# State-space layer: the input matrices of a pair of groups by one product of 128 rows, and value weights 424 bytes behind a multiple of 512

## The chip, the core and the metric

The kernel runs on one core of a Trainium2 chip. A core has a matrix engine (TensorE, in the profile PE; its weight loads are shown as PEld), a vector engine (VectorE, DVE), a scalar engine (ScalarE, ACT), GpSimd (POOL) and a queue that issues most DMAs (SyncE, SP). The engines run side by side and wait for each other on semaphores. Two memories matter: SBUF, 128 partitions wide, where operands lie, and PSUM, to which matmuls write and from which ACT or DVE copy the results away.

The metric is the device time of one launch in microseconds. A matmul multiplies a stationary operand (loaded first by LDWEIGHTS, partitions x columns) with a moving operand that streams through the array. A plain fp32 matmul stands in the trace as two MATMUL records and two LDWEIGHTS records; an fp32r matmul (a rounded format that the kernel uses for its high and low parts) stands as one of each.

## What is computed

Two residual layers over 512 tokens of width 1024. The first layer's mixer is a grouped state-space layer, the second's is attention with a forget gate; each is followed by a gated feed-forward part. The part of the reference that the change touches first is the state-space mixer: 64 groups of 16 channels, each with a complex diagonal state of 64.

```python
def s5_mixer(h, w_in, lam_re, lam_im, log_dt, b_re, b_im, c_re, c_im, d_skip, w_glu, w_out):
    u = h @ w_in
    ug = u.reshape(Bsz, S, S5_GROUPS, S5_GROUP)
...
    bb_re = k_re[..., None] * br - k_im[..., None] * bi
    bb_im = k_re[..., None] * bi + k_im[..., None] * br
...
        bu_re = jnp.einsum('blgc,gpc->blgp', u_c, bb_re)
        bu_im = jnp.einsum('blgc,gpc->blgp', u_c, bb_im)
...
        y = jnp.einsum('blgp,gcp->blgc', hs_re, cr) - jnp.einsum('blgp,gcp->blgc', hs_im, ci)
...
    y = y + d_skip.astype(f32) * u.astype(f32)
    y = jax.nn.gelu(y)
    y = y * jax.nn.sigmoid(y @ w_glu.astype(f32))
    return (y @ w_out.astype(f32)).astype(h.dtype)
```

The second part touched is the value projection of the attention, `v = proj[..., 2 * D_MODEL:3 * D_MODEL]`, together with the 16 forget logits that stand behind it.

## The kernel before

**The state-space layer.** The kernel does not scan token by token. It takes 8 tokens as one block (L = 8, so 64 blocks). Within a block the output is a small triangular (Toeplitz) product, and between blocks a scan over 64 steps carries the state. All of it is done for 8 groups at a time (GM = 8, 128 channels), in eight rounds m = 0 to 7. A round consists of:

- `inputs(m)`, lines 1163 to 1176: the projection u of these 128 channels, an fp32 product with 8 steps of 128x512 on PE (line 1169), a copy by ACT (line 1171), and a way through DRAM that turns its layout.
- `s5_inputs(m)`, lines 947 to 998: DVE makes the tile x (two products, lines 955, and a sum, line 959). On 128 partitions it holds a pair of groups, 64 states each: partitions 0 to 63 belong to group q, partitions 64 to 127 to group q + 4. PE then multiplies x with planes of the tile `rr` (line 971): two planes with the matrix C, and four planes with an identity matrix between them, so that one product both transposes x (the 64 columns that go to `w1`) and multiplies it with C (the 16 columns that go to `kt`). The real and imaginary part r = 0, 1 are accumulated in the 16 columns where they overlap. ACT copies the result from PSUM to `w1` (line 978) and `kt` (line 982), DVE adds the skip term to `kt` (line 983), `kt` goes to DRAM and comes back as a Toeplitz tile `tw` (lines 987 and 990), and ACT masks it into `t` (line 995).
- `s5_scan(m)`, lines 1000 to 1043: PE multiplies `w1` with u (line 1010), and DVE rotates, scans and rotates back (lines 1021 to 1042); ACT makes the scan's coefficients (line 1027).
- `s5_states_out(m)`, line 943, by `s5_outer` (line 935): DVE makes the matrices `w2` that read the states out, from `rr` too.
- `s5_outputs(m)`, lines 1045 to 1067: PE adds the products with `t` (line 1052) and with `w2` (line 1060), ACT applies the gelu (line 1066).

Beside these, PE makes the conditioning columns of this and the next sub-layer from weights that are streamed in (`ada_pe`, line 205), and from round 7 on the first four column tiles of the gate product (`glu_head`, line 1198).

The matmul of line 971 uses 64 partitions, one group at a time. `tile_position=(64 * g2, 0)` places it in the upper or lower half of the array, so that a product of the upper and one of the lower half can be under way together. For each pair of q (the loop over `a`), two PSUM tiles named `aux` are filled, one for each half. There are four `aux` tiles, and the scan, the outputs and the conditioning columns use them too. The tile x has one buffer, so DVE makes the next round's x only when line 971 has read the last one.

**What sets the order.** The start of the kernel, up to line 1159, stands in a block with a schedule by hand for PE, ACT, DVE and SP: there the order in the code is the order on each queue. `s5_planes` (line 805) and `s5_signs_c` (line 800) belong to it. Behind it the framework puts the instructions of each engine in an order, when the kernel is built, from their dependencies, its own costs and a few `issue_after` hints; on the chip each engine then works its queue in that order.

**The values of the attention.** `fox_values` (line 1322) multiplies the tokens with the value weights: here the activations are stationary and the weights move (line 1361), 256 columns for each of four parts q, and 272 for q = 0, which carries the forget logits. The weights are split by `split` into a high and a low part (lines 269 to 278). `part_of` (line 67) lays each part into a tile and leaves `aside` elements free in front of it. For the value weights that is VALUES, 16 elements or 64 bytes; other products use ASIDE, 22 elements or 88 bytes, for weights that are stationary.

Of the kernel before, what the change touches and what calls it, by code (L numbers as in the profile page):

```python
# [8 lines left out]
F32 = mybir.dt.float32  # L9
F32R = mybir.dt.float32r  # L10
I32 = mybir.dt.int32
AF = mybir.ActivationFunctionType
# [5 lines left out]
P = 128  # L18
# [4 lines left out]
G = 64  # L23
CG = 16
# [3 lines left out]
GM = P // CG  # L28
# [32 lines left out]
    pool.tile([P, n // 4], F32, name="fill", bufs=1)  # L61


ROOM, ASIDE, VALUES = 9 * P, 22, 16


def part_of(pool, shape, name, tag, bufs, aside=0):
# [714 lines left out]
class S5(Trunk):  # L782
# [16 lines left out]

    def s5_signs_c(self):  # L800
        nc = self.nc
        nc.scalar.activation(self.rr[:, 0], self.rr[:, 6], AF.Copy, scale=-1.0)
        return nc.scalar.activation(self.rr[:, 6], self.rr[:, 5], AF.Copy, scale=-1.0).ins

    def s5_planes(self, pool):
        nc = self.nc

        self.rr = pool.tile([P, 7, G // 2, CG], F32, name="s5_rr")
        eye = self.first["s5_eye"].rearrange("p (k c) -> p k c", c=CG)
        nc.scalar.activation(self.rr[:, 1:5], eye[:, :, None, :].to_broadcast([P, 4, G // 2, CG]), AF.Copy)  # L810
        self.z = self.dram.tile([KT, P + L - 1, CG * GM], F32, name="s5_z")
        self.causal = self.first["s5_causal"]
        self.mask = pool.tile([P, B], F32, name="s5_mask")
        nc.gpsimd.memset(self.mask, 1.0)
        nc.gpsimd.memset(self.mask[:, 0:1], 0.0)
# [124 lines left out]

    def s5_states_out(self, m):

        t1, t2 = self.s5_outer(m, self.er, self.rr[:, 5::-5], self.ei, self.rr[:, 0::6], ("w2", "x2"))
        self.nc.vector.tensor_tensor(t1, t1, t2, ALU.add)
        return t1

    def s5_inputs(self, m):

        nc, pool = self.nc, self.s5q

        qs = slice(m * (GM // 2), (m + 1) * (GM // 2))
        sh = [P, GM // 2, 2 * CG, L]
        x, x2 = (pool.tile([P, GM // 2, 2, CG, L], F32, name=n, bufs=1 if n == "x" else 2) for n in ("x", "x2"))
        for o, l, a in ((x, self.lr, 1), (x2, self.li, 0)):
            nc.vector.tensor_tensor(
                o.rearrange("p k r c j -> p k (r c) j"), l[:, qs, None, :].to_broadcast(sh),
                self.bb[:, qs, a:a + 2, :].rearrange("p k r c -> p k (r c)")[:, :, :, None].to_broadcast(sh), ALU.mult,
            )
        self.x_made = nc.vector.tensor_tensor(x, x, x2, ALU.add).ins
        w1 = pool.tile([P, GM, P], F32, name="w1", bufs=2)  # L960
        kt = pool.tile([P, CG, GM], F32, name="kt", bufs=2)
        dd = pool.tile([P, CG * GM], F32, name="dd", bufs=1)
        nc.sync.dma_start(dd, self.io["s5_dd"][m])
        for a in range(0, GM // 2, 2):
            ps = [self.aux.tile([P, 3, 160], F32, name="aux") for _ in range(2)]
            for j in range(2):
                q = m * (GM // 2) + a + j
                for r, (cols, planes) in enumerate(((slice(0, 80), slice(1, 6)), (slice(64, 144), slice(0, 5)))):
                    for g2 in range(2):
                        rows = slice(64 * g2, 64 * g2 + 64)  # L970
                        nc.tensor.matmul(  # L971
                            ps[g2][:, j, cols], x[rows, a + j, r].rearrange("p c j -> p (c j)"),
                            self.rr[rows, planes, q, :], start=(j == 0 and r == 0), stop=True,
                            tile_position=(64 * g2, 0), skip_group_check=True,
                        )
            for g2 in range(2):
                g = g2 * (GM // 2) + a
                nc.scalar.activation(
                    w1[:, g:g + 2, :].rearrange("p g (r x) -> p g r x", r=2),
                    ps[g2][:, :2].rearrange("p g (r x) -> p g r x", r=2)[:, :, :, :64], AF.Copy,  # L980
                )
                nc.scalar.activation(kt[:, :, g:g + 2].rearrange("p c g -> p g c"), ps[g2][:, :2, 64:80], AF.Copy)
        nc.vector.tensor_tensor(
            kt.rearrange("p c g -> p (c g)"), kt.rearrange("p c g -> p (c g)"), dd, ALU.add,
        )
        z = self.z[m]
        nc.sync.dma_start(z[:P], kt.rearrange("p c g -> p (c g)"))
        R = CG * GM
        tw = pool.tile([P, L, CG, GM], F32, name="tw", bufs=1)
        nc.sync.dma_start(  # L990
            tw.rearrange("p i c g -> p i (c g)"), bass.AP(z.tensor, z.offset, [[R, P], [R, L], [1, R]])
        )
        t = pool.tile([P, GM, CG, L], F32, name="t", bufs=3)
        for i in range(L):
            nc.scalar.activation(
                t[:, :, :, i].rearrange("p g c -> p c g"), tw[:, i], AF.Copy, scale=self.causal[:, i:i + 1]
            )
        return w1, t
# [76 lines left out]
    def s5(self, i, nxt):  # L1075
        nc, tc = self.nc, self.tc
# [4 lines left out]
        with ExitStack() as stack:  # L1081
# [7 lines left out]
            with ExitStack() as start:  # L1089
# [3 lines left out]
                def load_w(m):  # L1093
                    w[m] = self.raw([P, KT, P], self.io["s5_w_in"][m], m % 3)
# [6 lines left out]
                with tc.manual_schedule(engines={ENG.PE, ENG.Activation, ENG.DVE, ENG.SP}):  # L1101
# [3 lines left out]
                    ps = self.mm.tile([P, S], F32, name="mmp")  # L1105
# [4 lines left out]
                    rows = self.tmp.tile([P, S], F32, name="nm_t")  # L1110
# [6 lines left out]
                    scale = self.ada_pe(i, (1,), late=True)  # L1117
# [5 lines left out]
                    x = self.act.tile([P, KT, S], F32, name="a_x", tag="a_hi")  # L1123
# [6 lines left out]
                    ps = self.mm.tile([P, S], F32, name="mmp")  # L1130
# [8 lines left out]
                        nc.tensor.matmul(ps, w[0][:, k, :], x[:, k], start=(k == 0), stop=(k == KT - 1))  # L1139
                    next(shift)  # L1140
                    load_w(1)
                    nc.sync.dma_start(self.rr[:, 5:7], self.io["s5_c"])
                    nc.sync.dma_start(
                        self.z[:, P:, :].rearrange("m j r -> j m r"), zero[:, None, :].to_broadcast([L - 1, KT, CG * GM])
                    )
# [14 lines left out]
            pool = self.s5r = spool("s5r", stack)  # L1160
# [41 lines left out]
            ps = self.aux.tile([KT, P], F32, name="aux")  # L1202
            nc.tensor.transpose(ps, self.sc, self.ident)
            rows = self.tmp.tile([KT, P], F32, name="nm_h", bufs=4)
# [436 lines left out]
```

## Time and profile before

| what | us |
|---|---|
| median of three runs | 1230.08 |
| lowest, highest | 1227.98, 1237.5 |
| the profiled execution, its own time | 1229.46 |
| its span from first to last instruction | 1227.7 |
| PE busy in the span | 1192.7 (97%) |
| DVE busy | 1007.7 (82%) |
| ACT busy | 606.2 (49%) |
| state-space rounds on PE, line 971 first to last start | 48.2 to 158.5 |
| value products, line 1361 first to last start | 628.3 to 675.6 |

The table is from the first block of the profile's page, the list of runs, and the answers on the two source lines. A matmul record's duration is its whole way through the array, and records overlap, so busy time says little about how densely PE works. The chain of waits is of more use: it follows the work that ended last and gives to each piece the time until the next piece could start. The sums of the prediction are made from that view.

### The profile page before, as it was taken

The numbers are of one execution on the slowest core, as the hardware profiler recorded it, in microseconds if no ns is written. First come the engines' busy times: TensorE is split into PE (matmuls) and PEld (weight loads), VectorE is DVE, ScalarE is ACT, GpSimd is POOL, SyncE is SP. The second block draws the span as 40 slices with busy tenths as digits, with TensorE's granted clock in tenths as the row PEclk, the third lists the DMA queues.
The fourth block names the chain that finished last, engine by engine and source line by source line (L and its number), as shares of the span: only waits on it lengthen the run. The fifth ranks groups of instructions, "written<-read, shape, count | busy, mean of one in ns | idle before, by whom it ended". The sixth has DMA issues, their size and how long they took to land.

```text
span 1227.7 us, 20566 instructions
## 1 busy us (share of the span) xinstructions
PE 1192.7 (97%) x7921; PEld 1022.8 (83%) x7921; DVE 1007.7 (82%) x1872; ACT 606.2 (49%) x1137; POOL 82.7 (7%) x143
## 2 busy tenths in 40 slices
PE   7999999999999999999999999999999999999997
PEld 2466678898989899789899878778889999999987
DVE  7988886679899989799678588785899887888865
ACT  3543465336444543445443565654456554555543
POOL 0000000100000000000000333331000000000000
PEclk9999999999999999999989999999999999999999
DMA  9776678531354554453425444431313332233331
GB/s 353 241 247 215 223 220 282 192 133 44 129 173 162 189 161 154 157 174 116 144 104 205 167 135 145 156 123 62 113 47 107 119 119 91 101 104 108 108 99 69
DMA packets 74385, 183.83 MB, mean 150 GB/s; under 512 B 23231, under 2 KB 25631, under 8 KB 73263
## 3 DMA queue, kind: packets, MB, share of 16 engines
q1 hardware_dynamic: 68239, 161.02, 39.7%
q0 software_dynamic: 5760, 20.97, 5.2%
q8 instruction: 62, 1.02, 0.3%
q10 hardware_dynamic: 288, 0.52, 0.1%
q14 instruction: 36, 0.29, 0.1%
HBM read 175.57 MB, written 6.92 MB: 149 GB/s over the span
## 4 chain that ended last, share of the span: by engine, by line
PE 60%; issue 26%; DVE 8%; DMA 3%; POOL 1%; ACT 1%; SPq 0%; DVEq 0%; POOLq 0%; ACTq 0%
PE mmp L294 24%; PE mmp L550 10%; PE mmp L1169 4%; PE aux L550 4%; PE mmp L1361 2%; DVE w_lo L278 2%; PE aux L971 2%; PE mmp L1198 2%; POOL ada_raw L233 1%; PE aux L1060 1%; PE aux L1500 1%; PE mmp L205 1%; PE aux L1052 1%; DMA ada_raw<-in_ada_t 1%; PE mmp L1109 1%
## 5 line engine op out<-in xcount | busy, mean ns | idle before, releaser
L278 DVE TENSOR_TENSOR w_lo<-raw,w_hi 128x1024 fp32r<-128x1024 f32 (+4 forms) x173 | 183.3, 1065 | 31.7 <-ACT w_hi L277 31.3
L277 ACT ACTIVATE w_hi<-raw 128x1024 fp32r<-128x1024 f32 (+4 forms) x173 | 154.8, 905 | 100.7 <-PE mmp L294 48.2
L294 PE MATMUL mmp<-ghi,w_lo 128*128 128x512 f32 (+1 forms) x392 | 145.0, 370 | 0.9 <-DVE w_lo L278 0.7
L294 PE MATMUL mmp<-ghi,w_hi 128*128 128x512 f32 (+1 forms) x392 | 145.7, 372 | 0.0
L294 PE MATMUL mmp<-glo,w_hi 128*128 128x512 f32 (+1 forms) x392 | 145.2, 371 | 0.0
L294 PE MATMUL mmp<-a_hi,w_hi 128*128 128x512 f32 (+1 forms) x376 | 138.3, 370 | 1.5 <-ACT a_hi L433 1.5
L294 PE MATMUL mmp<-a_hi,w_lo 128*128 128x512 f32 (+1 forms) x376 | 136.1, 362 | 0.0
L294 PE MATMUL mmp<-a_lo,w_hi 128*128 128x512 f32 (+1 forms) x376 | 135.7, 362 | 0.0
L550 PE MATMUL mmp<-w_hi 128*128 128x256 f32 x396 | 110.1, 278 | 3.1 <-ACT nm_h L557 2.8
L550 PE MATMUL mmp<-w_hi,w_lo 128*128 128x256 f32 x396 | 110.0, 278 | 0.7 <-DVE w_lo L278 0.7
L550 PE MATMUL mmp<-w_lo,w_hi 128*128 128x256 f32 x396 | 109.9, 278 | 0.0
L557 ACT ACTIVATE nm_h<-mmp 128x256 f32<-128x256 f32 x99 | 37.2, 381 | 110.1 <-PE mmp L550 110.1
L278 DVE TENSOR_TENSOR w_lo<-sums,w_hi 128x1024 fp32r<-128x1024 f32 x74 | 90.1, 1219 | 0.0
L277 ACT ACTIVATE w_hi<-sums 128x1024 fp32r<-128x1024 f32 x74 | 77.0, 1054 | 22.2 <-DVE sums L518 20.2
L294 PEld LDWEIGHTS mmp<-ghi,w_lo 128*128 128x128 f32 x392 | 74.8, 191 | 14.3 <-DVE w_lo L278 1.9
L294 PEld LDWEIGHTS mmp<-ghi,w_hi 128*128 128x128 f32 x392 | 74.9, 191 | 11.7 <-ACT w_hi L277 0.4
L294 PEld LDWEIGHTS mmp<-glo,w_hi 128*128 128x128 f32 x392 | 74.8, 191 | 11.1
L294 PEld LDWEIGHTS mmp<-a_hi,w_hi 128*128 128x128 f32 x376 | 70.2, 188 | 13.8 <-issue 2.6
L294 PEld LDWEIGHTS mmp<-a_hi,w_lo 128*128 128x128 f32 x376 | 70.6, 188 | 12.0 <-DVE w_lo L278 1.0
L294 PEld LDWEIGHTS mmp<-a_lo,w_hi 128*128 128x128 f32 x376 | 70.7, 188 | 9.7
L362 DVE SCALAR_TENSOR_TENSOR h<-mmp,par,h 128x512 f32<-128x512 f32 (+1 forms) x100 | 68.0, 682 | 12.6 <-PE mmp L294 12.4
L550 PEld LDWEIGHTS mmp<-w_hi 128*128 128x128 f32 x396 | 74.8, 189 | 3.6 <-ACT nm_h L557 3.2
(317 smaller groups left out, 3084.7 us busy)
## 6 DMA issues: line engine op xcount, KB each, us to landing
raw<-in_w_up SPq DMA_DIRECT2D x88, 512.0 KB, 3.5
raw<-in_ada_w SPq DMA_DIRECT2D x40, 512.0 KB, 6.3
ada_raw<-in_ada_t POOLq DMA_DIRECT2D x40, 512.0 KB, 3.9
nf<-nfd SPq DMA_DIRECT2D x8, 1152.0 KB, 6.5
raw<-in_fox_qk SPq DMA_DIRECT2D x16, 512.0 KB, 4.0
raw<-in_w_down SPq DMA_DIRECT2D x24, 320.0 KB, 3.1
rawd<-in_w_down SPq DMA_DIRECT2D x24, 256.0 KB, 3.4
raw<-in_w_down SPq DMA_DIRECT2D x16, 384.0 KB, 3.4
```

Of the source, the lines that this page charges most:

```text
L205: self.last_mm = nc.tensor.matmul(ps[32 * qq:32 * qq + 32, :], self.sc32[:, k, :], w[:, q * S:(q + 1) * S], start=(step is steps[0]), stop ...
L233: (nc.gpsimd if late else nc.sync).dma_start(ws[n], src)
L277: nc.scalar.activation(hi, src, AF.Copy)
L278: return nc.vector.tensor_tensor(lo, src, hi.bitcast(F32), ALU.subtract)
L294: self.last_mm = self.nc.tensor.matmul(o, wt, xt[:, cols], start=(k == 0 and n == 0), stop=(k == nk - 1 and n == 2),)
L362: add = self.nc.vector.scalar_tensor_tensor(self.h[:, m, cols], ps, self.par[i][:, 16 + m:17 + m], self.h[:, m, cols], op0=ALU.mult, op1=A ...
L550: self.last_mm = nc.tensor.matmul(o, wt[:, k], xt[:, k], start=(first and k == 0 and n == 0), stop=(k == H - 1 and n == 2), skip_group_che ...
L557: a = nc.scalar.activation(t, o, AF.Copy)
L971: nc.tensor.matmul(ps[g2][:, j, cols], x[rows, a + j, r].rearrange("p c j -> p (c j)"), self.rr[rows, planes, q, :], start=(j == 0 and r = ...
L1169: nc.tensor.matmul(ps, w[m][:, k, :], x[:, k], start=(k == 0), stop=(k == KT - 1))
L1198: nc.tensor.matmul(gps[m], wt, xt[:, k], start=(k == 0 and part == 0 and xt is yhi), stop=(k == KT - 1 and part == 1))
L1361: self.last_mm = nc.tensor.matmul(ps[q, b][:, :n], xt[:, k, tb], wt, start=(k == 0 and i == 0), stop=(k == KT - 1 and i == 2),)
```

## The change

In `s5_inputs`, a pair of groups is multiplied in one product over all 128 partitions instead of two products over 64. So that the two groups stay apart, the moving operand gets two sets of columns: a tile `both` holds, for g2 = 0 and 1, the six planes with group g2's rows filled and the other group's rows zero. One matmul then streams 2 x 80 = 160 columns. The number of matmuls of a round falls from 16 to 8, each with its own LDWEIGHTS of 128 instead of 64 rows. Each q has one `aux` tile with both groups in it; ACT copies as many pieces of the same sizes as before (eight a round), in another cut.

The identity planes of the two `both` tiles, one for even and one for odd rounds, are written once at the start (`s5_planes`): POOL fills the tiles with zeros, and ACT copies the identity into each half, four copies of 64x256 elements for the one copy of 128x2048 before. The planes with C change with the round, so ACT copies them in each round: two copies of 64 partitions and 128 elements. `rr` loses its identity planes and is three planes (it was seven); its load, the sign changes and the read in `s5_states_out` follow.

VALUES becomes P - 22 = 106 elements, 424 bytes.

```diff
-ROOM, ASIDE, VALUES = 9 * P, 22, 16
+ROOM, ASIDE, VALUES = 9 * P, 22, P - 22
...
     def s5_signs_c(self):
-        nc.scalar.activation(self.rr[:, 0], self.rr[:, 6], AF.Copy, scale=-1.0)
-        return nc.scalar.activation(self.rr[:, 6], self.rr[:, 5], AF.Copy, scale=-1.0).ins
+        nc.scalar.activation(self.rr[:, 1], self.rr[:, 2], AF.Copy, scale=-1.0)
+        return nc.scalar.activation(self.rr[:, 2], self.rr[:, 0], AF.Copy, scale=-1.0).ins
...
-        self.rr = pool.tile([P, 7, G // 2, CG], F32, name="s5_rr")
+        self.rr = pool.tile([P, 3, G // 2, CG], F32, name="s5_rr")
         eye = self.first["s5_eye"].rearrange("p (k c) -> p k c", c=CG)
-        nc.scalar.activation(self.rr[:, 1:5], eye[:, :, None, :].to_broadcast([P, 4, G // 2, CG]), AF.Copy)
+        self.both = [pool.tile([P, 2, 6, GM // 2, CG], F32, name=f"s5_both{n}") for n in range(2)]
+        for t in self.both:
+            nc.gpsimd.memset(t, 0.0)
+            for g2 in range(2):
+                rows = slice(64 * g2, 64 * g2 + 64)
+                nc.scalar.activation(
+                    t[rows, g2, 1:5], eye[rows, :, None, :].to_broadcast([64, 4, GM // 2, CG]), AF.Copy
+                )
...
-        t1, t2 = self.s5_outer(m, self.er, self.rr[:, 5::-5], self.ei, self.rr[:, 0::6], ("w2", "x2"))
+        t1, t2 = self.s5_outer(m, self.er, self.rr[:, 0:2], self.ei, self.rr[:, 1:3], ("w2", "x2"))
...
-        for a in range(0, GM // 2, 2):
-            ps = [self.aux.tile([P, 3, 160], F32, name="aux") for _ in range(2)]
-            for j in range(2):
-                q = m * (GM // 2) + a + j
-                for r, (cols, planes) in enumerate(((slice(0, 80), slice(1, 6)), (slice(64, 144), slice(0, 5)))):
-                    for g2 in range(2):
-                        rows = slice(64 * g2, 64 * g2 + 64)
-                        nc.tensor.matmul(
-                            ps[g2][:, j, cols], x[rows, a + j, r].rearrange("p c j -> p (c j)"),
-                            self.rr[rows, planes, q, :], start=(j == 0 and r == 0), stop=True,
-                            tile_position=(64 * g2, 0), skip_group_check=True,
-                        )
-            for g2 in range(2):
-                g = g2 * (GM // 2) + a
-                nc.scalar.activation(
-                    w1[:, g:g + 2, :].rearrange("p g (r x) -> p g r x", r=2),
-                    ps[g2][:, :2].rearrange("p g (r x) -> p g r x", r=2)[:, :, :, :64], AF.Copy,
+        both = self.both[m % 2]
+        for g2 in range(2):
+            rows = slice(64 * g2, 64 * g2 + 64)
+            nc.scalar.activation(both[rows, g2, 0::5], self.rr[rows, 1::-1, qs], AF.Copy)
+        for q in range(GM // 2):
+            ps = self.aux.tile([P, 2, 160], F32, name="aux")
+            for r, (cols, planes) in enumerate(((slice(0, 80), slice(1, 6)), (slice(64, 144), slice(0, 5)))):
+                nc.tensor.matmul(
+                    ps[:, :, cols], x[:, q, r].rearrange("p c j -> p (c j)"), both[:, :, planes, q, :],
+                    start=(r == 0), stop=(r == 1), skip_group_check=True,
                 )
-                nc.scalar.activation(kt[:, :, g:g + 2].rearrange("p c g -> p g c"), ps[g2][:, :2, 64:80], AF.Copy)
+            gs = slice(q, GM, GM // 2)
+            nc.scalar.activation(
+                w1[:, gs, :].rearrange("p g (r x) -> p g r x", r=2),
+                ps.rearrange("p g (r x) -> p g r x", r=2)[:, :, :, :64], AF.Copy,
+            )
+            nc.scalar.activation(kt[:, :, gs].rearrange("p c g -> p g c"), ps[:, :, 64:80], AF.Copy)
...
-                    nc.sync.dma_start(self.rr[:, 5:7], self.io["s5_c"])
+                    nc.sync.dma_start(self.rr[:, 0::2], self.io["s5_c"])
```

## The prediction, made before the changed kernel ran

> **What bounds the kernel now.** I read the page's busy times first, then the stages from 41 to 164 us, in which the rounds of the state-space layer run, and then the chain of waits in that stretch.
>
> ```profile
> PE 1192.7 (97%) x7921; PEld 1022.8 (83%) x7921; DVE 1007.7 (82%) x1872; ACT 606.2 (49%) x1137; POOL 82.7 (7%) x143
> ```
>
> ```profile
> core 0: us, PE busy (x) PEld busy (x) DVE busy (x) ACT busy (x) POOL busy (x), PEclk, DMA share, GB/s
> 41.00:62.00 21.00, 21.00 (x143) 10.73 (x144) 19.98 (x29) 14.05 (x41) 0.00 (x0) 1.00 0.83 259
> 62.00:104.00 42.00, 41.92 (x343) 28.39 (x340) 36.03 (x61) 16.93 (x56) 0.00 (x0) 1.00 0.75 238
> 104.00:164.00 60.00, 59.84 (x498) 37.91 (x498) 49.77 (x77) 28.46 (x91) 0.00 (x0) 0.97 0.68 216
> ```
>
> ```profile
> by line: PE mmp L1169 43.8%; PE aux L971 19.6%; PE aux L1060 9.4%; PE aux L1052 9.4%; PE mmp L205 8.6%; PE aux L1010 6.6%; ACT w L978 0.9%; PE aux L162 0.8%; DVE m L1021 0.6%; ACT kt L982 0.3%; PE aux L157 0.3%; issue 0.2%
> ```
>
> The last row is the chain from 41.3 to 164 us, 122.7 us. PE is never idle there but for 1.2% in which the chain goes through ACT copies of line 978 and 982. So PE's own queue sets the end of this stage. DVE is close behind: it is idle for 1.0, 6.0 and 10.2 us of the three stretches. Line 971, which the change rewrites, is 19.6% of 122.7 = 24.0 us of the chain, and the two ACT pieces are 1.2% = 1.5 us.
>
> Next, one round and the first one in the same view (start, length, records of a piece):
>
> ```profile
> 48.24 1.95 PE aux L971 x32
> 50.19 3.63 PE mmp L1169 x8
> ...
> 62.33 1.93 PE aux L1052 x16
> 64.26 1.04 PE aux L971 x8
> 65.31 1.05 PE mmp L1169 x2
> 66.36 1.56 PE aux L971 x16
> 67.92 2.77 PE mmp L1169 x6
> 70.69 1.04 PE aux L971 x8
> 71.74 1.05 PE mmp L1169 x2
> 72.79 1.93 PE aux L1060 x32
> ...
> 141.64 4.49 PE mmp L1169 x10
> ...
> 153.98 1.05 PE aux L971 x8
> ```
>
> Three readings. (a) All 32 records of a round in one go take 1.95 us, two halves of the array at once. From round 2 on they fall into three groups with projection records (line 1169) between them, and then take 1.04 + 1.56 + 1.04 = 3.64 us: a group of 8 uses one half alone, at 0.13 us a record. (b) Six records of line 1169 take 2.77 us and two take 1.05, so one more costs (2.77 - 1.05)/4 = 0.43 us, and a piece between half-array groups carries 1.05 - 0.86 = 0.19 us on top: the array pays for going from halves to the whole and back. (c) Sixteen records on the whole array with 64 columns (line 1052) take 1.93 us, 0.12 each.
>
> **The product, part by part.** It removes 16 matmuls a round (32 records of 64 x 80 columns) and adds 8 (16 records of 128 x 160). The trace has no whole-array fp32 record of 160 columns. From 0.43 us for 512 columns, 160 take 160/512 x 0.43 = 0.134 us. The lower end is the 0.12 us of line 1052, which is what a record cannot go under; the upper end is twice the 1.95/16 = 0.122 us that an 80-column record takes on its half, 0.244, if doubled columns cost double. I take 0.134, since streaming is the same kind of work as in the 512-column row. A round is then 16 x 0.134 = 2.15 us, eight rounds 17.2 us (ends 15.4 and 31.2).
>
> Against that stand the 24.0 us of the groups, the 1.5 us of ACT pieces in the chain between groups, and the price of changing from halves to the whole. Fifteen pieces of line 1169 follow a group of line 971 in that stretch, the first at 50.19 and the last at 141.64; 15 x 0.19 = 2.9 us, of which I take 2.2, since some of these pieces run on into line 1060 or 205, which still use parts of the array. PE's part: 24.0 + 1.5 + 2.2 - 17.2 = 10.5 us less (ends 12.3 and -3.5).
>
> The Trainium skill, "TensorEngine Tiling (Array Packing)", Key Properties, says that a change of tiling mode drains the engine; the 0.19 us agrees. Its table of theoretical speedups speaks against this change: contractions of up to 64 rows gain up to 2x from two tiles that load and multiply in parallel. By that the eight rounds would cost up to 31 us and the kernel gain nothing; the chain agrees only for rounds 0 and 1.
>
> **PSUM and ACT.** Copies stay at eight a round, of the same sizes, and there are two more for the C planes:
>
> ```profile
> L995 ACT ACTIVATE t<-tw,first 128x128 f32<-128x128 f32 x56 | 18.0, 502 | 3.8 <-DMA tw<-s_z 3.8
> L978 ACT ACTIVATE w<-aux 128x256 f32<-128x256 f32 x32 | 12.3, 389 | 28.7 <-PE aux L971 28.5
> L982 ACT ACTIVATE kt<-aux 128x32 f32<-128x32 f32 x32 | 7.2, 226 | 0.0
> ```
>
> A q now takes PE 4 x 0.134 = 0.54 us and ACT 0.389 + 0.226 = 0.61 us. While the outputs hold two of the four `aux` tiles, the third q waits for the first copy: about 0.3 us in each of rounds 2 to 7, less where a record of line 1169 stands between. I take 1.5 us given back (ends 0 and 3). The two C copies, 16 in all at no more than 0.50 us each by line 995's row (same 128 elements), are 8 us of ACT work beside 59.4 of 123 us busy. They need only `rr` and the planes free since two rounds ago, so they lie hidden as long as nothing late is ahead of them on ACT's queue; that is a rival below.
>
> Round 0 is different, since `rr` is signed just before:
>
> ```profile
> 45.75 0.61 ACT L802 ACTIVATE s_rr<-s_rr 128x512 f32<-128x512 f32 x1
> 46.39 0.63 ACT L803 ACTIVATE s_rr<-s_rr 128x512 f32<-128x512 f32 x1
> 46.93 1.26 ACT L1027 ACTIVATE cf<-s_mask,s_mag 128x128 f32<-128x128 f32 x4
> 48.17 1.86 PEld L971 LDWEIGHTS aux<-s_rr,x 64*128 64x128 f32 x32 [0.76 <-DVE s_tab L922]
> ```
>
> The signs end at 47.0; two copies behind them end at about 47.8, before PE wants them at 48.2, or at about 49 if the coefficients of line 1027 stay ahead. Cost 0 to 0.8 us, taken 0.5. After line 971 the next on PE are the projections, and ACT's copies of `w1`.
>
> **DVE.** It waits for line 971 already (total us, times, longest):
>
> ```profile
> DVE x L955 <- PE aux L971: 8.9, 5, 2.8
> ...
> ACT t L995 <- DMA tw<-s_z: 3.8, 4, 1.7
> DVE kt L983 <- ACT kt L982: 3.7, 2, 2.8
> ```
>
> x has one buffer, so the split groups hold back the next x for 8.9 us in total, and the late copies hold `kt` for 3.7. One short run of line 971 shortens both, so DVE can follow PE for most of the gain. In 62 to 104 us it has only 6.0 us idle, though, and PE's gain there is about 4; I take off 1.5 us (ends 0 and 6).
>
> **The start and the load.** POOL zero-fills two tiles of 128x768, ACT copies the identity in four pieces of 64x256:
>
> ```profile
> 26.35 0.33 SPq L1142 DMA_DIRECT2D s_rr<-in_s_c  x1
> ```
>
> ```profile
> 1.71 0.16 POOL L814 MEMSET s_mask<- 128x64 f32 x1
> ...
> 2.87 1.89 ACT L810 ACTIVATE s_rr<-first 128x2048 f32<-128x2048 f32 x1
> ...
> 5.52 1.15 ACT L1108 ACTIVATE nm_t<-h 128x512 f32<-128x512 f32 x2 [0.76 <-DMA h<-in_x]
> ```
>
> Twelve times 0.16 bounds a fill at 1.9 us, probably much less; four copies by 0.389 (line 978's row, 256 elements) are 1.6 us against 1.89. ACT is idle 0.76 us before the first square, which waits for x from DRAM. Taken 0 (ends 0 and 1, if both fills are slow). The load of C has the same bytes in two pieces a partition and is issued at 26.35, 19 us before the signs: 0. Edits of `s5_states_out` only change the plane: 0.
>
> **The value weights.** Rows of the chain, and of the groups by shape (the number after the comma is the mean ns of one record):
>
> ```profile
> 635.40 5.71 PE mmp L1361 x47
> ...
> 659.74 1.13 DVE w_lo L278
> ...
> 664.30 11.57 PE mmp L1361 x96
> ```
>
> ```profile
> 1125.57 2.72 PE mmp L550 x24
> ```
>
> ```profile
> L550 PE MATMUL aux<-a_hi,w_hi 128*128 128x256 f32 x132 | 36.5, 276 | 0.0
> L1361 PE MATMUL mmp<-w_hi,a_hi 128*128 128x256 f32 x96 | 26.6, 281 | 0.4 <-DVE v L278 0.4
> L1520 PE MATMUL aux<-plo,v 128*128 128x256 f32 x32 | 8.4, 286 | 0.0
> ```
>
> The last part, q = 3, takes 11.57/96 = 0.1205 us a record; the feed-forward's line 550 with the same shape takes 2.72/24 = 0.1133. In line 550 the stationary weights lie 88 bytes behind a multiple of 512 and the moving operand on one; in line 1361 the moving weights lie 64 behind. With 424 = 512 - 88 the two operands stand to each other as in line 550. So 96 records could save 0.7 us, and the 192 of q = 0 and 1, which mix 256 and 272 columns at 5.71/47 = 0.1215 where line 550's rate would give 0.117, another 0.9. The 96 of q = 2 lie beside DVE work (659.74). Ends: a gain of 1.6; a loss of 288 x 5 ns = 1.4, if it became like line 1520. I take a gain of 0.9. The Trainium skill, "TensorE: Matmul & The Clock Gate", Part 2, step 1, says that the moving operand and the weight load have separate read ports, so loading steals nothing; by that the term is 0, and no run here shows which.
>
> **The sum.** 10.5 - 1.5 - 0.5 - 1.5 + 0.9 = 7.9 us less. The profiled execution took 1229.46 us, 1.76 more than its span and 0.6 below the median of 1230.08. Forecast: 1229.46 - 7.9 = 1221.5 us. All that follows at 164 us (scan and outputs of round 7, gate product) begins earlier by the same amount.
>
> **Rivals.**
> - All of it arrives. Only the copies' pacing is partly hidden and DVE follows: 10.5 + 1.6, 1217.4 us or a little less. For it: 8.9 us of DVE's idle time is put down to line 971 itself. Against: 6.0 us of idle DVE in 62 to 104.
> - DVE becomes the bound. Its order then sets the rounds, and only some 3 us come through: 1226.5 us. For it: 36.03 of 42 us busy.
> - The doubled columns cost double (0.244 us a record): -3.5 - 2 + 0.9, 4.6 us more, 1234 us. Against: records of 64 and 80 columns both take 0.12, so a record is not paid by its columns there. The table of the Trainium skill's "TensorEngine Tiling (Array Packing)" amounts to this case.
> - Slower. PE in rounds 1 to 7 waits for a C copy that stands on ACT's queue behind line 995 of the round before, which itself waits for `tw`: up to 8 copies of 0.32 (18.0/56) = 2.6 us plus 1.7 of wait, 4.3 us seven times = 30 us, less 11.4: 1248 us. It passes 1% from 3.4 us a round on ((12.3 + 11.4)/7). Against: the copies can go a round earlier.
>
> **How the numbers follow.** Forecast 0.52, all of it 0.16, DVE 0.20, double 0.08, slower 0.04. One per cent, about what a measurement of this kernel can tell from no change, is 12.3 us: faster means below 1217.8, slower above 1242.4. Faster holds most of the first rival, 0.14; slower 0.04; within 1% the rest, 0.82. The range 1216 to 1229 holds the forecast, the DVE case and over half of the first rival, 0.82 or so.
>
> **What would show it.** Line 971 has 128 records (16 a round) at 0.13 us in the chain, in runs of near 2.2 us, and line 1169's records between stay at 0.43. The wait of x on line 971 falls from 8.9 us to under 4. Line 1361's last 96 records take 10.9 us. Round 7's line 971, now at 153.98, starts 6 to 10 us earlier. It is wrong if line 971 costs over 0.2 us a record, if PE's weight loads wait for ACT's new copies, or if DVE passes 95% in 62 to 164 us with the end unmoved.

## The result, and the profile after

The changed kernel took 1216.21 us in the median of six runs (1213.14 to 1218.12), beside 1229.42 us for the kernel before; the ratio is 0.9878 with a 95% interval of 0.9849 to 0.9908. The profiled execution took 1217.02 us. So the change is worth about 13 us, 1.2%, where 7.9 us were forecast: the sign was right, the size was too small, and "within 1%", which was given the largest chance, did not hold. The time itself lies just inside the lower end of the stated range (1216 to 1229).

In the changed kernel the new product stands in line 978 (it was 971), and lines behind it are moved: 1169 is 1174, 1010 is 1015, 1052 is 1057, 1060 is 1065, 1198 is 1203, 1361 is 1366, 955 is 962, 983 is 988, 1187 is 1192. ACT's copies out of PSUM, 978 and 982, are now 983 and 987.

The stages from 41 to 164 us of the changed kernel, with the columns as before:

```profile
41.00:62.00 21.00, 21.00 (x103) 11.46 (x104) 19.76 (x29) 16.22 (x49) 0.00 (x0) 1.00 0.78 246
62.00:104.00 42.00, 41.47 (x321) 27.59 (x316) 38.91 (x67) 22.10 (x75) 0.00 (x0) 1.00 0.82 266
104.00:164.00 60.00, 59.52 (x553) 39.91 (x551) 57.19 (x88) 33.60 (x97) 1.28 (x2) 1.00 0.79 251
```

DVE does more in the same time: 57.19 of the last 60 us, where it had 49.77. One round in the chain of waits (start, length, records):

```profile
96.54 1.93 PE aux L1057 x16
98.47 0.60 PE aux L978 x4
99.06 0.86 PE mmp L1174 x2
99.92 0.54 PE aux L978 x4
100.47 1.72 PE mmp L1174 x4
102.18 1.09 PE aux L978 x8
103.27 1.72 PE mmp L1174 x4
104.99 1.93 PE aux L1065 x32
```

Four records of 160 columns take 0.54 us, 0.135 each, and a round takes 0.60 + 0.54 + 1.09 = 2.23 us instead of 3.64. The round is still cut into three, because the PSUM tiles still come free one by one, but the cuts cost next to nothing now: two projection records between two groups take 0.86 us, where the same two took 1.05, and four take 1.72 = 4 x 0.43. Only the first group of a round takes 0.06 us more than 0.54.

How far ahead the kernel is at the end of the stage shows where the gate product goes over to its fifth column tile. First the row of before, then that of after:

```profile
197.58 5.45 PE aux L294 x24
```

```profile
186.34 5.45 PE aux L294 x24
```

That is 11.24 us of the 12.5 by which the two spans differ. Part of it is the clock. In the profile of before, PE had half its clock for 3.4 us in the rounds and for 3.4 us in the feed-forward part, which the changed kernel's profile has not; the busy times inside the two stretches of before, PEclk third from the end:

```profile
104.10:107.30 3.20, 3.20 (x5) 1.14 (x5) 3.07 (x6) 2.71 (x12) 0.00 (x0) 0.50 1.07 335
537.60:540.80 3.20, 3.20 (x17) 3.20 (x16) 1.60 (x4) 0.76 (x2) 0.06 (x1) 0.50 0.70 233
```

A third, of 6.8 us at 616.0, has its like in the changed kernel, at 602.8. A stretch of 3.4 us at half clock costs up to 1.7 us, so these two profiles owe up to 3.4 us of their difference to these two stretches, 1.7 of it in the rounds.

The waits of DVE between 41 and 172 us, in the form shown before:

```profile
DVE x L962 <- PE aux L978: 2.7, 3, 1.1
DVE a_lo L1192 <- ACT a_hi L1191: 1.5, 3, 0.9
DVE kt L988 <- ACT kt L987: 1.2, 2, 1.0
```

The wait of x fell from 8.9 to 2.7 us, that of `kt` from 3.7 to 1.2.

### The profile page after: what moved, and what is told of

It is laid out like the page before. It is cut to its first block, busy times and chain, and to the rows that moved or that the text cites. A ratio compares the mean times of both kernels' runs of the same rounds, so it can differ in the third digit from the quotient of the medians.

```text
span 1215.2 us, 20334 instructions
## 1 busy us (share of the span) xinstructions
PE 1180.3 (97%) x7793; PEld 1015.4 (84%) x7793; DVE 1007.6 (83%) x1872; ACT 609.8 (50%) x1156; POOL 83.9 (7%) x145
## 4 chain that ended last, share of the span: by engine, by line
PE 56%; issue 26%; DVE 8%; DMA 5%; ACT 2%; POOL 2%; SPq 0%; POOLq 0%; DVEq 0%; ACTq 0%
PE mmp L294 24%; PE mmp L550 11%; PE aux L550 4%; PE mmp L1366 3%; PE mmp L1174 2%; DVE w_lo L278 2%; PE mmp L1203 2%; POOL ada_raw L233 1%; PE aux L1505 1%; DMA ada_raw<-in_ada_t 1%; PE aux L1065 1%; PE mmp L1114 1%; PE aux L1057 1%; PE aux L978 1%; DMA yt<-s_yd 1%
## 5 line engine op out<-in xcount | busy, mean ns | idle before, releaser
L294 PEld LDWEIGHTS mmp<-ghi,w_hi 128*128 128x128 f32 x392 | 74.7, 191 | 11.5 <-ACT w_hi L277 0.2
L362 DVE SCALAR_TENSOR_TENSOR h<-mmp,par,h 128x512 f32<-128x512 f32 (+1 forms) x100 | 68.0, 681 | 12.1 <-PE mmp L294 11.9
```

What stands on the lines that cost most here:

```text
L294: self.last_mm = self.nc.tensor.matmul(o, wt, xt[:, cols], start=(k == 0 and n == 0), stop=(k == nk - 1 and n == 2),)
L362: add = self.nc.vector.scalar_tensor_tensor(self.h[:, m, cols], ps, self.par[i][:, 16 + m:17 + m], self.h[:, m, cols], op0=ALU.mult, op1=A ...
```

## The experiments

All times are medians, and the ratios are to runs of the kernel before on the same chip. Below, "the product alone" is the changed kernel with VALUES back at 16.

A run also lists its mean granted clock c. If every drop is to one half, as all that the traces show are, (1 - c) x span is at most what drops cost it. "Without half clock" below is the mean time less this estimate. The kernel before comes to 1218.7 to 1220.0 us by it on the four chips used, the product alone (e1) to 1209.1.

**One part alone.** First the product without the other value offset, then the offset without the product.

```diff
 changed kernel:
-ROOM, ASIDE, VALUES = 9 * P, 22, P - 22
+ROOM, ASIDE, VALUES = 9 * P, 22, 16
```

> The product of 128 rows alone, the value weights back at 64 bytes. Theory P (PE's own queue: the gain is time that line 971 and the changes between half and whole array took, 24.0 + 1.5 + 2.2 us of the chain against 17.2): the whole gain or a little more, ratio 0.987 to 0.989 to the kernel before, and the value products at the old pace, 0.1205 us a record in the last part, less than 0.1205 in the first. Rival V (the value weights bring a part): the gain is smaller by 1 us or more, 0.990 or above.

Measured: 1216.92 us, ratio 0.9882 (0.985 to 0.9914). The whole gain is the product's, within what runs differ.

```diff
 kernel before:
-ROOM, ASIDE, VALUES = 9 * P, 22, 16
+ROOM, ASIDE, VALUES = 9 * P, 22, P - 22
```

> The value weights at 424 bytes alone, the product as before. Theory P: no gain. The traces of before and after show the records of 256 columns start 113 to 118 ns apart before and 120 ns apart after, so 0 to 1 us slower, ratio 1.000 to 1.001. Rival V: 1 us or more faster, 0.999 or below. The clock: if the half-array groups are what lets the granted clock drop at 104 us in the profile of before, a drop of 3.4 us stands in the rounds here too; if drops come at random, it is elsewhere or missing.

Measured: 1228.37 us, ratio 0.9988 (0.9966 to 1.001). The interval takes in 1, so the time alone cannot settle half a microsecond; the records can. The chain in the value products, first of the changed kernel and then of the product alone:

```profile
622.40 5.82 PE mmp L1366 x47
```

```profile
626.06 5.71 PE mmp L1366 x47
...
655.24 11.57 PE mmp L1366 x96
```

With 64 bytes the lengths are those of before to the hundredth; with 424 the same 47 records take 0.11 us more. The profile of e2 has a half-clock stretch of 3.4 us at 41 us and none among the half-array groups from 48 us on, so these groups can run without one.

**The product in another form.** Here the two ingredients, records of 160 columns and no change of array mode, are taken apart.

```diff
 product alone:
-                nc.tensor.matmul(
-                    ps[:, :, cols], ..., both[:, :, planes, q, :],
-                    start=(r == 0), stop=(r == 1), skip_group_check=True,
-                )
+                for g2 in range(2):
+                    nc.tensor.matmul(
+                        ps[:, g2, cols], ..., both[:, g2, planes, q, :],
+                        start=(r == 0 and g2 == 0), stop=(r == 1), skip_group_check=True,
+                    )
```

> Whole-array products with the zero rows, but one group at a time: 80 columns, 16 matmuls a round, value weights at 64 bytes. No change of array mode, and no halves. Theory P by record time: 32 records of 0.112 us are 3.6 us a round instead of 2.15, so 11 to 12 us of PE more than the changed kernel, and the kernel lands at 1225 to 1229 us (ratio 0.997 to 1.001). Rival S (the changes of array mode are the main cost, and records hardly count): 1216 to 1220 us, ratio 0.99 to 0.992.

Measured: 1229.22 us, ratio 0.9979 (0.9965 to 0.9994), as theory P by record time had it. Its chain has this group where the changed kernel takes 1.09 us (x8 above) for the same work, and DVE waits for it:

```profile
73.03 1.76 PE aux L979 x16
```

```profile
DVE x L962 <- PE aux L979: 15.0, 5, 7.3
```

Sixteen records of 80 columns take 1.76 us, 0.11 each: a record of 80 columns on the whole array costs not much less than one of 160 does (0.135). Losing the change of mode alone gains next to nothing if the records double.

```diff
 kernel before:
-            ps = [self.aux.tile([P, 3, 160], F32, name="aux") for _ in range(2)]
+            ps = [self.mm.tile([P, 3, 160], F32, name="mmp") for _ in range(2)]
```

> The kernel before with one edit: the PSUM tiles of line 971 come from the other pool, so that they do not wait for the outputs' tiles. The half-array products of a round then stand together, 32 records in 1.95 us as in rounds 0 and 1. Theory P: most of the gain without the zero planes, since 1.95 us and one change of mode a round (0.4) are near the 2.15 of the changed kernel: 1216 to 1221 us, ratio 0.989 to 0.993. Rival H (half-array products are slow in themselves, whatever their grouping): 1226 us or more. Against both stands that the other pool's tiles are needed by the projections, which could wait for them: then above 1229.

Measured: 1223.96 us, ratio 0.9951 (0.9917 to 0.9985), between the two theories. The half-array products do run as pairs again in some rounds:

```profile
85.94 1.95 PE mmp L971 x32
...
101.09 2.75 PE mmp L971 x32
```

So 6 of the 13 us are to be had without the zero planes, by PSUM tiles that are free in time: the split groups were most of the cost of line 971, not the half array in itself. Counted from the start of each PE record to the start of the next, up to the gate product's fifth column tile, line 971 owns 25.7 us before, 19.8 in e4, and its successor 18.8 after the change. What keeps e4 from the rest is only in part known: in five of the eight rounds part of the 32 records still follow each other singly, 0.11 us apart, instead of in pairs (2.75 us), a change of mode remains in every round, and lines 1010 and 1052 own 2.1 us more than before; from 136 us on its chain leaves PE for DVE and DRAM.

**Is PE still the bound?** More and less work for PE, then for DVE.

```diff
 product alone:
-                nc.tensor.matmul(
-                    ps[:, :, cols], ...
+                for _ in range(2 if r == 0 else 1):
+                    nc.tensor.matmul(
+                        ps[:, :, cols], ...
```

> The changed product (value weights at 64 bytes) with the first of each two matmuls issued twice; the second overwrites the first, so the result is the same. That is 8 records of 0.134 us a round more, 8.6 us of PE in eight rounds. Theory P (PE is still the bound of the rounds): 8 to 9 us over the product alone, about 1226 us, ratio 0.995 to 0.997. Rival D (with the product shorter, DVE is the bound, at 57.19 of 60 us busy between 104 and 164): at most 4 us over it, 1221 or less, ratio up to 0.992.

Measured: 1228.86 us, 11.9 more than the product alone (ratio 0.9994, 0.9966 to 1.0021). All of the added 8.6 us arrives and some more, also without half clock (1219.6 against 1209.1). Rival D, at most 4 us, is out.

```diff
 product alone, in inputs(m):
-                    for k in range(KT):
-                        nc.tensor.matmul(ps, w[m][:, k, :], x[:, k], start=(k == 0), stop=(k == KT - 1))
+                    for k in range(KT - 1):
+                        nc.tensor.matmul(ps, w[m][:, k, :], x[:, k], start=(k == 0), stop=(k == KT - 2))
```

> The changed product (value weights at 64 bytes) with the projection of rounds 1 to 7 over seven of eight steps; one eighth of that sum is left out. PE has 7 x 2 records of 0.43 us less, 6.0 us. Theory P: 5 to 6 us under the product alone, 1211 to 1212 us, ratio 0.983 to 0.985. Rival D: at most 2 us under it, 1215 or more.

Measured: 1218.72 us, ratio 0.9918 (0.9882 to 0.9953), no gain over the product alone. Without half clock it is 1207.4 us, 1.6 of the 6.0 us. Nor does DVE's wait for the buffer matter:

```diff
 product alone: x with bufs=2 in s5_inputs and in s5_outer
```

> The changed product (value weights at 64 bytes) with two buffers for x, so that DVE need not wait for line 978 to have read the last x. In the trace after, DVE waits 2.7 us for that in all (8.9 us before the change). Theory P: no more than 1 us under the product alone, 1216 to 1218. Rival D: those 2.7 us come through, 1214 to 1215.

Measured: 1219.72 us, ratio 0.9929 (0.9903 to 0.9956), if anything slower, with and without half clock (1212.2); both theories expected it at or under the product alone.

```diff
 product alone and kernel before, in s5_states_out:
-        self.nc.vector.tensor_tensor(t1, t1, t2, ALU.add)
+        self.nc.gpsimd.tensor_tensor(t1, t1, t2, ALU.add)
```

> The changed product (value weights at 64 bytes) with one DVE instruction a round moved to POOL, the sum that ends the state-out matrices (line 951 of the changed kernel, 1.22 us each, 9.8 us of DVE in eight rounds). Taking 6.0 us from PE gave only 1.6 us, so theory D' (after the change DVE stands directly behind PE) expects that both must shrink: this edit alone 0 to 3 us under the product alone, 1214 to 1218. If DVE alone is the bound now: 5 us or more under it, 1212 or less. If POOL is slow at it, or DVE slows down beside it: above 1218.

> The kernel before with the same edit. Theory P (before the change PE alone is the bound): no gain, 1228 to 1231 us, ratio 0.998 to 1.002. Rival D (DVE was the bound before, and the change gained by freeing DVE): 4 us or more, ratio 0.997 or below.

Measured: 1231.67 us (ratio 1.0022, 1.0001 to 1.0042) and 1242.68 us (1.0113, 1.0081 to 1.0144). Both lost, and the pair tells nothing about DVE, since POOL needs 3.5 us for what DVE does in 1.22. Its group in e10, and two stages of e11:

```profile
L951 POOL TENSOR_TENSOR w<-w,x 128x1024 f32<-128x1024 f32 x8 | 28.1, 3508 | 140.3 <-DVE x L942 97.4 <-DVE w L942 28.5 <-PE mmp L205 14.4
```

```profile
62.00:104.00 42.00, 38.67 (x312) 25.76 (x308) 33.52 (x51) 16.23 (x54) 8.57 (x4) 0.88 0.63 200
104.00:164.00 60.00, 59.07 (x430) 38.67 (x427) 47.45 (x68) 22.60 (x75) 8.26 (x3) 0.89 0.66 206
```

The granted clock is 0.88 and 0.89 in these two stages, and PE is idle for 3.3 us in the first. By the estimate, half clock makes 12.5 of the 14.6 us that e11 lost to the kernel before, and 4.0 of the 14.8 that e10 lost to the product alone. So the sum was left out instead.

```diff
 e12: product alone; e13: kernel before; e14: e6, in s5_states_out:
-        self.nc.vector.tensor_tensor(t1, t1, t2, ALU.add)
```

> The changed product (value weights at 64 bytes) without the DVE sum that ends the state-out matrices: its second term is left out, 8 x 1.22 = 9.8 us of DVE less, nothing else moved. The run with that sum on POOL could not tell, since POOL took 3.5 us each and stood in the way. Theory D' (after the change PE and DVE stand close behind each other, so relief of one alone gives little): 0 to 3 us under the product alone, 1214 to 1218. If DVE alone is the bound after the change: 5 to 9 us, 1208 to 1212.

> The kernel before, with the same sum left out. Theory P (before the change PE alone is the bound): 0 to 2 us, 1227 to 1231 us. Rival D (the change gained by freeing DVE): 4 us or more, 1226 or less.

> The changed product with both reliefs: the DVE sum left out (9.8 us of DVE) and the projection of rounds 1 to 7 over seven of eight steps (6.0 us of PE). Alone the projection gave 1.6 us in time without the half-clock share. Theory D': together they give 5 to 7 us, 1210 to 1213 us, clearly more than the sum of the two alone. If neither engine is the bound after the change (latency of the way through DRAM sets the rounds): 3 us or less.

Measured: e12 1218.26 us (ratio 0.9914, 0.9881 to 0.9947), e13 1232.44 us (1.0013, 0.9994 to 1.0032), e14 1224.62 us (0.9948, 0.9929 to 0.9967). In total time, 9.8 us less for DVE give nothing before the change, as theory P said; after it, relief of DVE gives nothing, relief of PE gives nothing, and both together are worse than either. But the clock stands in the way of this reading. One stage of e13, in which PE is hardly idle:

```profile
104.00:164.00 60.00, 59.77 (x432) 36.67 (x430) 42.42 (x68) 24.83 (x80) 0.00 (x0) 0.90 0.65 200
```

The mean clock of e13 is 0.987, beside 0.991 for the kernel before on its chip, and without half clock e13 takes 1215.6 us against 1219.2, so 3.6 us less. That is near the 4 us of rival D: before the change, part of what DVE was spared did reach PE (line 971 itself owns 23.5 us in e13, without half clock, instead of 25.7), and the lower clock took it away again. So e13 does not show that PE alone was the bound. e14 has a half-clock stretch of 17.1 us at 157 us; without half clock it takes 1209.4, e12 1210.0 and e6 1207.4 us, beside 1209.1 for the product alone. So after the change neither relief brings more than 1.6 us by this count either, and both together nothing. Theory D', a pair of engines close behind each other, falls with that. DVE's share in e12 shows how idle it may be without effect:

```profile
104.00:164.00 60.00, 58.98 (x546) 39.42 (x547) 49.52 (x80) 32.36 (x95) 1.28 (x2) 1.00 0.80 250
```

What else could set the end of the stage may stand in the chain of the changed kernel, from 138 us on:

```profile
145.27 3.00 DMA yt<-s_yd
...
150.90 6.21 DMA yt<-s_yd
...
157.13 1.18 ACT a_hi L1191
...
158.34 1.24 DVE a_lo L1192
```

It waits 9.2 us for outputs that come back from DRAM, between pieces of ACT and DVE. PE is busy all the while, though (59.52 of 60 us above), with other work that it has to do anyway. That this way is the new limit was not tried by itself, and every kernel here also had its queues put in a new order when it was built, which may move a few microseconds either way (e7 is 3 us slower for a mere buffer). It stays open.

**Where the value weights lie, and the clock.**

```diff
 e8, product alone:
-ROOM, ASIDE, VALUES = 9 * P, 22, 16
+ROOM, ASIDE, VALUES = 9 * P, 22, 0
 e9, product alone:
-ROOM, ASIDE, VALUES = 9 * P, 22, 16
+ROOM, ASIDE, VALUES = 9 * P, 22, 64
```

> The changed product with the value weights at a multiple of 512 bytes. To be read is the pace of the value products' records of 256 columns: 117.6 ns in mean with 64 bytes, 119.7 with 424. If what counts is how many 512-byte pieces a row of the moving operand touches (three with 64 and 424, two with 0): 113 to 115 ns. If what counts is that both operands start alike (as in line 1525 of the changed kernel, where both start at a multiple of 512): 119 to 121.

> The changed product with the value weights at 256 bytes behind a multiple of 512. To be read is the pace of the value products' records of 256 columns. With 64 bytes it was 117.6 ns, with 0 and with 424 it was 119.7. If the place of the moving row within 512 bytes sets it and half-way is best: 113 to 116 ns; if it is only 64 that differs: 119 to 120. The total should equal the product alone within 1 us.

Measured: e8 1212.23 us in its one run, e9 1213.66 us (ratio 0.9876, 0.9846 to 0.9905), level with the changed kernel's runs. The ratio of e9 is that of the product alone within 0.001. The value products of e9 by shape, then those of the product alone:

```profile
L1366 PE MATMUL mmp<-w_lo,a_hi 128*128 128x256 f32 x96 | 26.9, 282 | 0.0
```

```profile
L1366 PE MATMUL mmp<-w_lo,a_hi 128*128 128x256 f32 x96 | 26.6, 279 | 0.0
```

Taking the starts of successive records of 256 columns, the mean distance is 119.7 ns with 0 bytes, 119.6 with 256, 119.7 with 424 and 117.6 with 64. The same 64 bytes give 116.3 in the kernel before, and 115.9 to 117.8 over all twelve kernels that have them. Of the four places, only 64 is better, and of the two rules that e8 set against each other neither is left: the number of 512-byte pieces does not count (119.7 with 0 bytes), and a like start of the operands is not special either (119.6 with 256).

The changed kernel once more, unedited:

> The changed kernel itself, beside the kernel before on the same chip, to part two things in the first comparison: the mean time at half clock cost the kernel before about 10.4 us a run (clock 0.9916 of 21 runs) and the changed one 6.9 (0.9943 of 6). Theory P with chance in the clock: time without that cost 10 to 11 us lower, the cost itself the same in both within 1.5 us, ratio 0.990 to 0.992. Rival C (the change itself makes the clock drop less): cost again 3 us or more lower, ratio 0.987 to 0.989.

Measured: 1216.46 us beside 1228.04, ratio 0.9898 (0.987 to 0.9926). The estimate of what drops cost is 10.3 us for the kernel before (67 runs beside the experiments, mean 1229.8 us) and 7.3 us for the changed kernel (12 runs, mean 1216.4). Without half clock the means are 1219.5 and 1209.1: about 10.4 us are the work, and about 3.0 of the 13.4 us are fewer or shorter drops. a1's own numbers are those of theory P, chance in the clock: 10.8 us without half clock, and 1.3 us for the clock's part (9.0 to 7.7). But one comparison does not show it: the clock's part varies from 1.3 to 3.5 us between comparisons, and whether the change causes it or chance does stays open. PE's idle time does not settle it: e10 and e11 have it and a low mean clock (0.990 and 0.983), but e13 has a low clock (0.987) with PE busy for 101.6 of 102 us between 62 and 164.

No version here beats the changed kernel by more than runs differ.

## Why the prediction was right in sign and too small

What each line owns of PE's time, from the start of each record to the start of the next, from 41.3 us on (111 projection records in both) to the first record of the fifth column tile:

| us | before | after |
|---|---|---|
| the product, line 971, then 978 | 25.73 | 18.84 |
| projections, line 1169, then 1174 | 53.46 | 49.82 |
| line 1052, then 1057 | 15.31 | 14.80 |
| lines 1010 and 1198, then 1015 and 1203 | 32.24 | 31.82 |
| all others | 29.12 | 29.12 |

That is 11.5 us less, and the half-clock stretch at 104 us, which fell on projections, is 1.7 of it. So the rounds gained 9.8 us of work, where the forecast had 10.5 - 1.5 - 0.5 - 1.5 = 7.0.

- **Bound.** Right in the main. 8.6 us more for PE (e5) cost 11.9. That PE alone was the bound before is not shown: without half clock, 9.8 us less for DVE brought 3.6 (e13).
- **Record price.** Right: 0.134 us taken, 0.135 measured. The rival by which doubled columns cost double is out. The lower end, 0.12 us as what a record cannot go under, was not one: a record of 80 columns takes 0.11 us on the whole array (e3). The Trainium skill, "TensorEngine Tiling (Array Packing)", Theoretical Speedup, gives up to 2x for a dimension of up to 64. The traces agree where both halves are fed: 32 records of 80 columns take 1.95 us on two halves and 3.53 us on the whole array (e3). In rounds 2 to 7 they were not always both fed, and the 32 records took 3.64 us in round 2.
- **Change of array mode.** Right: 2.2 us taken; the projections own 3.6 us less, of which 1.7 is the clock, so 1.9, and line 1052, whose last record stood before a half-array group, 0.5.
- **PSUM pacing.** Right in size: 1.5 us taken; line 978 owns 18.8 us, 1.6 more than its 128 records at 0.135 us, 17.3. Not all of that is waiting for copies: 0.06 us a round stand at the first record behind line 1057.
- **Round 0.** 0.5 us taken, about 0.1 measured (PE starts line 978 at 48.29, line 971 at 48.17). The order put ACT's C copies ahead of the scan coefficients:

```profile
47.14 1.29 ACT L974 ACTIVATE s_both<-s_rr 64x128 f32<-64x128 f32 x4
...
48.29 2.34 PE L978 MATMUL aux<-s_both,x 128*128 128x160 f32 x16
```

- **DVE.** Of the forecast's own terms this is the step whose mechanism failed. I took off 1.5 us because DVE had only 6.0 us of idle time in 62 to 104. But 4.5 of these 6.0 us were themselves a wait for line 971. With the groups short, DVE's waits for x and `kt` shrank from 12.6 to 3.9 us between 41 and 172 us, so DVE moved forward with PE. PE and its weight loads wait for DVE for 2.8 us there after, 3.3 before. So nothing of the 1.5 us was measured: the deduction counted a symptom of the old bound as a limit of the new one.
- **Start and load.** Right: the first square starts at 5.54 us after, 5.52 before.
- **Value weights.** Wrong in sign. A gain of 0.9 us was taken from the likeness to line 550; the records became slower, 119.7 ns instead of 116.3 in the kernel before and 117.6 in the product alone, some 0.6 to 1.0 us over 288 records. It went to the lower end, towards line 1520. The Trainium skill, "TensorE: Matmul & The Clock Gate", Part 2, step 1, says that loading weights takes no read bandwidth from the running matmul; it says nothing of where the operands start. Here 2 to 3 ns a record depend on that; why stays open.
- **The clock.** The other step that failed, and the largest: the sum has no term for it, though the row of 104 to 164 us that the prediction shows has a granted clock of 0.97. It is up to 3.4 us of the two profiles' difference, and about 3.0 us over all runs.

Together: 7.9 forecast; 1.5 from DVE, 0.4 from round 0, 0.2 from the change of mode, 0.1 from the product and 0.4 in lines 1010 and 1198, which no run takes apart, and 1.5 to 1.9 less from the values, make 8.6 to 9.0. The two profiles differ by 12.5 - 3.4 = 9.1 without the two half-clock stretches. Over all runs 10.4 remain without half clock, a little more than this account finds; the clock brings the rest to 13.

The first rival, "all of it arrives", at 1217.4 us, had a chance of 0.16 and came nearest in the total, but by luck. It was right that DVE follows. It also had a gain of 1.6 us from the values, which was a loss, and its sum had no cost of pacing, which came. The clock, for which it had no term either, made up for both.

The slower rival did not come: no wait of PE's weight loads on line 974 is in the trace. But the C copies were not quite hidden. Five of them stand in the changed kernel's chain between 47.14 and 51.81 us, which goes on through ACT, DVE and DRAM and comes back to PE at 70.13 us. The projection record before that owns 1.07 us instead of 0.43, so this path cost about 0.6 us, once.

Of the signs that were named, these came: 0.135 us a record and 2.23 us a round for line 978, 0.43 us for the projections between, 2.7 us of wait for x, and round 7's first record of the product at 143.99 us, 10.0 earlier. DVE is busy for 96.1 of 102 us between 62 and 164 us, 94%. The value products did not come down to 10.9 us: the starts of their last 96 records span 11.5 us, 11.3 before.

## What to carry to other kernels

Products on half the array were cheap here only while both halves were fed (1.95 us a round against 3.64). Where their PSUM tiles come free one at a time, one product over the whole array with zero rows can be faster (2.23 us), and it stands between other whole-array work at next to no cost of changing over. Before taking off for the next engine in line, see what its idle time is a wait for: if it waits for the very work that becomes shorter, it may follow. Read the granted clock beside every time: of 13 us here about 3 came with the clock, and e13 gave back to it all that it had saved.

## What the runs showed of the hardware that was not expected

- A whole-array fp32 record of 80 columns takes 0.11 us (e3), one of 160 columns 0.135 (the changed kernel): twice the columns for a quarter more time.
- POOL needs 3.5 us (e10; 3.2 in e11) for a sum of 128x1024 fp32 elements for which DVE needs 1.22, and used in the rounds it went with a kernel 15 us slower (e10 against the product alone, e11 against the kernel before), part of it half clock.
- Of four places of the moving row within 512 bytes, three give records 119.6 to 119.8 ns apart (five kernels) and one, 64 bytes, 115.9 to 117.8 (twelve kernels).
